# Weight sums of each pair's last product queued behind an earlier split on VectorE, in all pairs but the last gated one

## The chip, the cores and the metric

The kernel runs on one core of a Trainium2 chip. A time is the device time of one execution in microseconds, of the slowest core where there are several; here there is one. TensorE (PE, with its weight loads PEld), VectorE (DVE), ScalarE (ACT) and GpSimd (POOL) each take their instructions in a fixed order; SyncE (SP) issues nearly all transfers (DMAs), also in a fixed order. An instruction waits at the head of its engine's queue until what it needs is there, and everything behind it on that engine waits too.

## What is computed

One layer of a decoder over 512 tokens of width 2048, all in float32:

```
p = rms_norm(x) @ w_in                       # 2048 x 6160
A = gated linear attention (4 heads, chunks of 64)
B = dilated sliding-window attention (8 heads, three dilations)
x = x + concat(A, B) @ w_out                 # 2048 x 2048
h = rms_norm(x)
x = x + (silu(h @ w_gate) * (h @ w_up)) @ w_down    # 2048 x 5632 twice, 5632 x 2048
```

Nearly all of the work is in the large products with weights that stand in memory: w_in, w_out, w_gate, w_up and w_down.

## The kernel before

**Products.** The large products are made by a fast scheme with seven products instead of eight for each two-by-two block: P1, P5, P6, P3, P7, P2 and P4 in this order. A *pair* is one such block product: two column blocks of 512 of a weight (or of w_gate and w_up), with 2048 rows (1408 for the last third of w_down). Its weight is cut in quarters named a, b, c, d; each quarter is loaded in four *groups* (g = 0 to 3; three in the last two pairs) of 128 x 1024 elements, 512 KB. P1, P3 and P2 use the quarters a, d and c as they are. P5, P6, P7 and P4 need differences, which VectorE writes over one of the two: P5 makes a = b - a, P6 makes a = d - a, P7 makes b = d - b, and P4 makes a = c - a. I call each of these 128 x 1024 subtractions a *sum*, after the code. They are line 230, in `Pair.source`.

**Splits.** Float32 products are made of a high and a low part of both factors. For each *item* (one product, one group) ScalarE casts the weight tile to its high part `wh` (line 320), VectorE subtracts that to get the low part `wl` (line 324, the *split*), and TensorE then runs twelve matmuls of 128 x 512 (line 364): eight on `wh`, then four on `wl`. `wh` and `wl` have two buffers each. So a pair has 28 items, 28 casts, 28 splits and 16 sums.

**The stream.** `stream` runs over the items of 24 pairs: four pairs of the input projection, one gated pair of it, two pairs with w_out, eleven pairs with w_gate and w_up (the gated pairs, j = 0 to 10), and six pairs with w_down. I number them 0 to 23: 0 to 4 w_in, 5 and 6 w_out, 7 to 17 w_gate and w_up, 18 to 23 w_down. (A pair before these is written out by hand.) At item k it traces the cast of item k+1, the sum of item k+2 and the split of item k+1, then the matmuls of item k. Work of other kinds (attention, the norm, the factors of the next stage) is traced between the matmuls in small steps, by `step`.

**Who sets the order.** That is only the order in which the program is traced. A scheduler then sets the order on each engine, and issues an instruction early when its inputs are there by the scheduler's own reckoning. A sum of P4 needs the quarter c, whose load needs a free one of the twelve weight buffers, and the quarter a after the split of P6. So the scheduler puts it as much as ten splits ahead of its own item's split: among the splits of P3 and P7, where it is traced among those of P2. `tc.issue_after(ins)` tells the scheduler to place what is traced in a block behind `ins` on that engine; it sets the order alone and adds no semaphore. Before the change it is used in one place around the sums: in the gated pair of the input projection (pair 4), whose sums stay behind the latest step of the attention's softmax (`behind_heads`).

**Buffers.** Sixteen weight tiles of a pair go through the twelve buffers of `wpool`: the four c tiles take the buffers of d, and b of the next pair takes those of c. A c tile is free when both the split of P2 and the sum of P4 have read it, an a tile after the split of P4. The load of the next tile waits for that at the head of SyncE's queue.

**Handover from pair 6 to pair 7.** Pair 6 makes the last columns of `x` after attention. VectorE adds the residual (lines 277 and 1445), ScalarE squares and scales it (1478, 1453), TensorE transposes it (1166), ScalarE copies it out (1177), SyncE stores it to `xn_d` (1181) and loads it back as `top` and `r` (1227, 1281), and from these VectorE and ScalarE make the factors `AA` and `AS` (178, 179) of pair 7. The third item of pair 7, (P1, group 2), needs the factor made of the first `top`.

Of the kernel before, what the change touches and what calls it, by code (L numbers as in the profile page):

```python
# [2 lines left out]

# [28 lines left out]
PRODUCTS = ("P1", "P5", "P6", "P3", "P7", "P2", "P4")  # L32
# [76 lines left out]
def block_kernel(ctx: ExitStack, tc: tile.TileContext, ins, out):  # L109
    nc = tc.nc  # L110
# [18 lines left out]
    def nm(s):  # L129
        uid[0] += 1  # L130
        return f"{s}_{uid[0]}"
# [34 lines left out]
    class Operand:  # L166


        def __init__(self, groups):
            self.groups = groups  # L170
            self.t = {}
# [16 lines left out]
    def folded(w):  # L188

        return w.rearrange("p (b a) -> p a b", b=2)  # L190
# [8 lines left out]
    class Pair:  # L199


        def __init__(
            self, op, rows, w1, w2, final, step, scale=None, before=None, products=PRODUCTS
        ):
            self.op, self.rows, self.w1, self.w2 = op, rows, w1, w2
            self.final, self.step, self.scale, self.before = final, step, scale, before
            self.q, self.dst, self.held = {}, {}, {}
            self.products = products
            self.closes = {**CLOSES}
            if products is FIRST_CLOSED:  # L210
                self.closes["P1"] = self.closes.pop("P2")
# [7 lines left out]
        def source(self, prod, g):  # L219

            if prod in SINGLE:
                t = self.quarter(SINGLE[prod], g)
                if prod == "P2" and self.products is FIRST_CLOSED:
                    self.q.pop(("c", g))
                return t
            one, two = SUMS_OF[prod]
            src = self.quarter(two, g)
            minuend = self.quarter(one, g)
            with self.behind_heads():
                nc.vector.tensor_tensor(src, minuend, src, op=ALU.subtract)  # L230
            return src

        def behind_heads(self):

            if self.final is final_gate and "head" in recent:
                return tc.issue_after(recent["head"])
            return ExitStack()

        def accs(self):
# [51 lines left out]
        def end(self, prod):  # L291
# [6 lines left out]
            else:  # L298
                self.held[prod] = self.seeds(src, int(prod == "P5"))

    def stream(pairs):


        items, asks = [], {}
        for p in pairs:
            for part in p.products:
                groups = [int(g) for g in part[3:] or "0123"[: p.op.groups]]
                if groups[-1] == p.op.groups - 1:
                    asks[len(items)] = p
                items += [(p, part[:2], g) for g in groups]  # L310
        last = len(items) - 1
        sources, high, low = {}, {}, {}

        def total(k):
            p, prod, g = items[k]
            sources[k] = p.source(prod, g)

        def first_part(k):
            high[k] = hpool.tile([P, 2, 512], F32R, name=nm("wh"), tag="wh")
            nc.scalar.copy(high[k], sources[k])  # L320

        def second_part(k):
            low[k] = hpool.tile([P, 2, 512], F32R, name=nm("wl"), tag="wl")
            nc.vector.tensor_tensor(  # L324
                low[k], sources.pop(k), high[k].bitcast(F32), op=ALU.subtract
            )

        def ensure(k):

            p, prod, g = items[k]  # L330
            finish(lambda: (COMBO[prod], g) in p.op.t)

        total(0)
        first_part(0)
        total(1)
        second_part(0)
        for k, (p, prod, g) in enumerate(items):
            if g == 0:
                if prod == p.products[0] and p.before:
                    p.before()  # L340
                p.begin(prod)
            if k in asks:
                p.ask(prod)
            now[0] = k
            run_soon()
            ensure(min(k + 1, last))
            if k < last:
                first_part(k + 1)
            if k + 2 <= last:
                total(k + 2)  # L350
            if k < last:
                second_part(k + 1)
            a = p.op.t[COMBO[prod], g]
            fresh = prod in ("P1", "P5", "P2")
            h, l = high.pop(k), low.pop(k)
            order_ = [
                (m, w, terms, jj, hl)
                for w, terms in ((h, (0, 1)), (l, (0,)))
                for jj in range(2) for m in range(2) for hl in terms
            ]  # L360
            if k == last:
                order_.sort(key=lambda o: o[0])
            for i, (m, w, terms, jj, hl) in enumerate(order_):
                nc.tensor.matmul(  # L364
                    p.dst[prod][m], a[:, jj, hl, m * P : (m + 1) * P], folded(w[:, jj, :]),
                    start=fresh and g == 0 and len(terms) == 2 and jj == 0 and hl == 0,
                    stop=g == p.op.groups - 1 and len(terms) == 1 and jj == 1,
                    skip_group_check=not fresh,
                )
                if i == 7:  # L370
                    p.step()
            if g == p.op.groups - 1:
                p.end(prod)
# [7 lines left out]
    def run_soon():  # L381
        for d in list(soonest):
            d[0] -= 1
            if d[0] <= 0:
                soonest.remove(d)
                d[1]()
# [120 lines left out]
    def step(n=1):  # L507
        for d in list(deferred):
            d[0] -= 1
            if d[0] <= 0:  # L510
                deferred.remove(d)
                d[1]()
        if any(d[2] for d in deferred):
            return
        spent = 0.0
        while spent + 1e-6 < n:
            if spent:
                run_soon()
            cost = advance()
            if cost is None:  # L520
                break
            spent += cost
        return spent
# [19 lines left out]
    def finish(ready):  # L543

        while not ready():
            hurry[0] = True
            run_soon()
            assert advance() is not None
        hurry[0] = False

    def paced(counts):
        counts = iter(counts)
        return lambda: step(next(counts, 1))
# [67 lines left out]
    def bias_tables():  # L621


        rel = work("T", (33, 8))
        nc.gpsimd.memset(rel[32:33, :], 1.0)
        load(rel[0:32, :], ins["rel_bias"])
        parts = []
        for c0, cn, t0, t1 in ((0, 512, "v", "qT"), (512, NB - 512, "oT", "kT")):
            oh = work(t0, (33, cn))
            load(oh, ins["onehot"][:, c0 : c0 + cn])  # L630
            parts.append((c0, cn, oh, t1))
        yield
        yield
        for c0, cn, oh, t1 in parts:
            bp = bank()
            nc.tensor.matmul(bp[:8, :cn], rel, oh, start=True, stop=True)
            lv = work(t1, (8, cn))
            nc.vector.tensor_copy(lv, bp[:8, :cn])
            store(bias_d[:, c0 : c0 + cn], lv)
        yield  # L640
        load(rep_d, bass.AP(tensor=bias_d.tensor, offset=0, ap=[[NB, 8], [0, P], [1, NB]]))
        yield
# [759 lines left out]
    def pair(*args, **kw):  # L1402
        pairs.append(Pair(*args, **kw))

    pair(opx, rows_in, col(1536), col(1024), final_proj("va1", "va0"), rate((22, 1), (6, 0.6)),
         row_scale, before=lambda: background.extend([gates(), bias_tables()]))
# [5 lines left out]
         products=FIRST_CLOSED)  # L1412
# [256 lines left out]
    def before_ffn(j):  # L1669
        if j == 10:  # L1670
            background.append(down_jobs(0))

    for j in range(11):
        c = slice(512 * j, 512 * j + 512)
        pair(
            opn, rows_n, w_gate[:, c], w_up[:, c], final_ffn(j),
            paced(paces.get(j, ())), tok_scale, before=lambda j=j: before_ffn(j),
        )


# [46 lines left out]
    for i in range(3):  # L1727
        g0 = 4 * i
        rows_d = [(512 * (g0 + g), 512 * (g0 + g) + 256) for g in range(opd[i].groups)]
        for np_ in range(2):  # L1730
# [5 lines left out]
                before=(lambda i=i: background.append(down_jobs(i + 1))) if lead else None,  # L1736
# [6 lines left out]
    for engine in ("act", "dve", "pe"):  # L1743
        behind.enter_context(tc.issue_after(recent[engine]))
    pairs[1].before = behind.close
    stream(pairs)
    drain()

# [34 lines left out]
```

## Time and profile before

| what | value |
|---|---|
| median of 3 runs | 1935.62 us (1932.67 to 1936.36) |
| the profiled execution's own time | 1928.62 us |
| its span, first to last instruction | 1926.8 us |
| granted TensorE clock, mean | 0.999 |
| TensorE busy | 1900.7 us (99%) |
| VectorE busy | 1684.6 us (87%) |
| ScalarE busy | 1070.6 us (56%) |
| transfers | 362.01 MB, 188 GB/s over the span |

The profiled execution took 1928.62 us, 1.8 us more than its span and 7.0 us less than the median. A matmul's busy time is longer than its share of the engine: matmuls are pipelined, so 99% busy hides short gaps, and one has to look at the starts. The timeline merges equal neighbours: "x8" is eight instructions, with the start of the first and the time until the last has ended, and in brackets the idle time of the engine before them with what ended it. VectorE's 128 x 1024 instructions are shown with 1.22 us, but follow each other 1.14 us apart.

### The profile page before, as it was taken

The page shows a single profiled execution, that of the slowest core. Times are in us where ns is not written, and L with a number is a line of the kernel's source. Part 1 is how long each engine was busy: PE and PEld are TensorE (multiplying, and loading weights), DVE is VectorE, ACT ScalarE, POOL GpSimd, SP SyncE. Part 2 cuts the span into 40 slices and gives each one's busy share as a digit, 9 for nine tenths or more (in the row PEclk, how much of TensorE's full clock was granted, in tenths as well). Part 3 has the DMA queues.
Part 4 walks back from the last instruction along what each step waited for, and adds up shares of the span by engine and source line. Part 5 has one row for each costly group of instructions (what it writes and reads, how often), then busy time and mean ns, then how long its engine had stood idle before and what let it go on. Part 6 is the DMA issues. An engine that isn't in the chain of part 4 may idle for free.

```text
span 1926.8 us, 25472 instructions
## 1 busy us (share of the span) xinstructions
PE 1900.7 (99%) x8986; PEld 1642.7 (85%) x8986; DVE 1684.6 (87%) x1915; ACT 1070.6 (56%) x1550; POOL 58.0 (3%) x80
## 2 busy tenths in 40 slices
PE   8999999999999999999999999999999999999999
PEld 7888888888888878888888888888888888888887
DVE  8997887877999799978878879879879989989987
ACT  8564564567776676544544444544446546546543
POOL 1000221010000010000000000000000000000000
PEclk9999999999999999999999999999999999999999
DMA  8458365476767594564564554564556785955761
GB/s 284 132 167 277 102 190 153 137 209 196 221 228 245 188 310 158 154 191 147 154 191 144 151 186 132 158 190 123 166 184 188 215 283 175 277 205 173 247 219 66
DMA packets 341800, 362.01 MB, mean 188 GB/s; under 512 B 132790, under 2 KB 202623, under 8 KB 341672
## 3 DMA queue, kind: packets, MB, share of 16 engines
q1 hardware_dynamic: 341320, 360.17, 59.6%
q8 instruction: 70, 1.15, 0.2%
q14 instruction: 58, 0.48, 0.1%
q10 hardware_dynamic: 352, 0.21, 0.0%
HBM read 298.16 MB, written 64.51 MB: 188 GB/s over the span
## 4 chain that ended last, share of the span: by engine, by line
PE 68%; DVE 11%; issue 3%; DMA 3%; ACT 1%; POOL 0%; DVEq 0%; SPq 0%; ACTq 0%; POOLq 0%
PE acc L364 66%; DVE wl L324 5%; DVE wa L230 2%; DVE AS L179 1%; PE bank L1033 1%; PE bank L999 1%; DVE wb L230 1%; ACT wh L320 0%; DVE AA L179 0%; DMA wc<-in_w_gate 0%; PE bank L1026 0%; DVE seed L281 0%; DMA top<-xn_d 0%; DMA r<-xn_d 0%; DMA x_d<-seed 0%
## 5 line engine op out<-in xcount | busy, mean ns | idle before, releaser
L364 PE MATMUL acc<-wh,AS 128*128 128x512 f32 x3008 | 710.9, 379 | 0.0
L364 PEld LDWEIGHTS acc<-wh,AS 128*128 128x128 f32 x3008 | 568.3, 189 | 81.1 <-issue 0.2
L320 ACT CAST wh<-wa 128x1024 fp32r<-128x1024 f32 x376 | 394.0, 1049 | 400.3 <-PE acc L364 369.7
L364 PE MATMUL acc<-wh,AA 128*128 128x512 f32 x2256 | 535.8, 380 | 2.1 <-ACT wh L320 1.8
L324 DVE TENSOR_TENSOR wl<-wa,wh 128x1024 fp32r<-128x1024 f32 x376 | 456.8, 1217 | 53.0 <-ACT wh L320 46.1
L364 PEld LDWEIGHTS acc<-wh,AA 128*128 128x128 f32 x2256 | 426.8, 189 | 64.6 <-ACT wh L320 3.3
L364 PE MATMUL acc<-wl,AS 128*128 128x512 f32 x1504 | 398.0, 386 | 7.3 <-DVE wl L324 7.1
L364 PEld LDWEIGHTS acc<-wl,AS 128*128 128x128 f32 x1504 | 279.5, 189 | 60.5 <-DVE wl L324 20.0
L364 PE MATMUL acc<-wl,AA 128*128 128x512 f32 x1128 | 295.1, 384 | 1.7 <-DVE wl L324 1.5
L364 PEld LDWEIGHTS acc<-wl,AA 128*128 128x128 f32 x1128 | 211.3, 189 | 36.4 <-DVE wl L324 6.4
L320 ACT CAST wh<-wb 128x1024 fp32r<-128x1024 f32 x94 | 98.6, 1048 | 125.3 <-PE acc L364 108.5
L320 ACT CAST wh<-wc 128x1024 fp32r<-128x1024 f32 x94 | 98.4, 1047 | 113.1 <-PE acc L364 108.7
L230 DVE TENSOR_TENSOR wa<-wc,wa 128x1024 f32<-128x1024 f32 x94 | 114.5, 1222 | 49.6 <-DMA wc<-in_w_gate 30.1
L320 ACT CAST wh<-wd 128x1024 fp32r<-128x1024 f32 x94 | 98.5, 1048 | 99.1 <-PE acc L364 96.9
L324 DVE TENSOR_TENSOR wl<-wc,wh 128x1024 fp32r<-128x1024 f32 x94 | 114.6, 1219 | 35.8 <-ACT wh L320 34.3
L324 DVE TENSOR_TENSOR wl<-wd,wh 128x1024 fp32r<-128x1024 f32 x94 | 114.4, 1220 | 16.2 <-ACT wh L320 11.9
L324 DVE TENSOR_TENSOR wl<-wb,wh 128x1024 fp32r<-128x1024 f32 x94 | 113.6, 1217 | 6.7 <-ACT wh L320 6.5
L230 DVE TENSOR_TENSOR wa<-wb,wa 128x1024 f32<-128x1024 f32 x94 | 113.5, 1219 | 2.0 <-DMA wb<-in_w_down 1.1
L230 DVE TENSOR_TENSOR wb<-wd,wb 128x1024 f32<-128x1024 f32 x94 | 114.6, 1219 | 0.6
L230 DVE TENSOR_TENSOR wa<-wd,wa 128x1024 f32<-128x1024 f32 x94 | 112.9, 1219 | 0.0
L281 DVE SCALAR_TENSOR_TENSOR seed<-acc,rs,seed 128x512 f32<-128x512 f32 x96 | 70.5, 746 | 23.3 <-PE acc L364 23.3
L265 ACT ACTIVATE seed<-acc,rs 128x512 f32<-128x512 f32 x96 | 60.6, 680 | 0.8 <-PE acc L364 0.8
(309 smaller groups left out, 1313.2 us busy)
## 6 DMA issues: line engine op xcount, KB each, us to landing
wa<-in_w_gate SPq DMA_DIRECT2D x44, 512.0 KB, 3.8
wb<-in_w_up SPq DMA_DIRECT2D x44, 512.0 KB, 4.5
wd<-in_w_up SPq DMA_DIRECT2D x44, 512.0 KB, 3.5
wc<-in_w_gate SPq DMA_DIRECT2D x44, 512.0 KB, 3.4
wc<-in_w_in SPq DMA_DIRECT2D x32, 512.0 KB, 4.1
wa<-in_w_in SPq DMA_DIRECT2D x24, 512.0 KB, 5.8
wb<-in_w_in SPq DMA_DIRECT2D x24, 512.0 KB, 5.7
wd<-in_w_in SPq DMA_DIRECT2D x24, 512.0 KB, 6.5
```

Source lines behind the costliest of these rows:

```text
L179: nc.vector.tensor_tensor(low, src, high.bitcast(F32), op=ALU.subtract)
L230: nc.vector.tensor_tensor(src, minuend, src, op=ALU.subtract)
L265: nc.scalar.activation(halves(t), unfolded(src[m]), AF.Copy, scale=self.scale(half, m))
L281: nc.vector.scalar_tensor_tensor(halves(seed[m]), unfolded(src[m]), self.scale(half, m), halves(seed[m]), op0=ALU.mult, op1=ALU.add,)
L320: nc.scalar.copy(high[k], sources[k])
L324: nc.vector.tensor_tensor(low[k], sources.pop(k), high[k].bitcast(F32), op=ALU.subtract)
L364: nc.tensor.matmul(p.dst[prod][m], a[:, jj, hl, m * P : (m + 1) * P], folded(w[:, jj, :]), start=fresh and g == 0 and len(terms) == 2 and ...
L999: nc.tensor.matmul(lp[:, :n], qh[:, b * P : (b + 1) * P], kh[:, :n], start=True, stop=True)
L1033: nc.tensor.matmul(op, vh[:, k, :], lgs[b][:, k * P : (k + 1) * P], start=(k == 0), stop=(k == b))
```

## The change

The splits of the stream are remembered in a queue of six. When a sum of P4 is traced for item k+2, the oldest of these six is the split of item k-5, seven items up the stream from the sum's own. The sum is now placed behind that split in VectorE's order. The gated pair of the input projection keeps its own rule, and the pair with j = 10, the last of w_gate and w_up (pair 17), is left out with `runs_ahead`. No instruction, load or buffer is added or removed.

```
+    splits = deque(maxlen=6)
...
         def second_part(k):
             low[k] = hpool.tile([P, 2, 512], F32R, name=nm("wl"), tag="wl")
-            nc.vector.tensor_tensor(
+            splits.append(nc.vector.tensor_tensor(
                 low[k], sources.pop(k), high[k].bitcast(F32), op=ALU.subtract
-            )
+            ).ins)
...
-            with self.behind_heads():
+            with self.held_back(prod):
                 nc.vector.tensor_tensor(src, minuend, src, op=ALU.subtract)
             return src
 
-        def behind_heads(self):
+        def held_back(self, prod):
 
             if self.final is final_gate and "head" in recent:
                 return tc.issue_after(recent["head"])
+            if prod == "P4" and not self.runs_ahead and len(splits) == splits.maxlen:
+                return tc.issue_after(splits[0])
             return ExitStack()
...
     for j in range(11):
         c = slice(512 * j, 512 * j + 512)
         pair(
             opn, rows_n, w_gate[:, c], w_up[:, c], final_ffn(j),
             paced(paces.get(j, ())), tok_scale, before=lambda j=j: before_ffn(j),
+            runs_ahead=j == 10,
         )
```

In the order of the built program, the four sums of P4 of a gated pair stood 10 splits ahead of their own items' splits, behind the splits of (P3, 1), (P3, 2), (P3, 3) and (P7, 0); they now stand 6 ahead, behind (P7, 1), (P7, 2), (P7, 3) and (P2, 0). The scheduler moves other instructions with them: in pair 6 the last two sums stand only 2 and 1 splits ahead of their own, and what feeds pair 7 is reordered on VectorE, ScalarE, TensorE and SyncE. In pairs 4, 5, 7 and 17 the places of the sums stay as they were.

More of the change, by code (lines that the diff above doesn't have):

```diff
@@ L1 @@
 import math
+from collections import deque
 from contextlib import ExitStack
@@ L202, in __init__ @@
         def __init__(
-            self, op, rows, w1, w2, final, step, scale=None, before=None, products=PRODUCTS
+            self, op, rows, w1, w2, final, step, scale=None, before=None, products=PRODUCTS,
+            runs_ahead=False,
         ):
@@ L208, in __init__ @@
             self.products = products
+            self.runs_ahead = runs_ahead
             self.closes = {**CLOSES}
@@ L228, in source, with held_back @@
             minuend = self.quarter(one, g)
-            with self.behind_heads():
+            with self.held_back(prod):
                 nc.vector.tensor_tensor(src, minuend, src, op=ALU.subtract)
             return src
-        def behind_heads(self):
+        def held_back(self, prod):
             if self.final is final_gate and "head" in recent:
                 return tc.issue_after(recent["head"])
+            if prod == "P4" and not self.runs_ahead and len(splits) == splits.maxlen:
+                return tc.issue_after(splits[0])
             return ExitStack()
@@ L299, in end @@
                 self.held[prod] = self.seeds(src, int(prod == "P5"))
+    splits = deque(maxlen=6)
     def stream(pairs):
@@ L323, in second_part @@
             low[k] = hpool.tile([P, 2, 512], F32R, name=nm("wl"), tag="wl")
-            nc.vector.tensor_tensor(
+            splits.append(nc.vector.tensor_tensor(
                 low[k], sources.pop(k), high[k].bitcast(F32), op=ALU.subtract
-            )
+            ).ins)
         def ensure(k):
@@ L1677, in block_kernel @@
             paced(paces.get(j, ())), tok_scale, before=lambda j=j: before_ffn(j),
+            runs_ahead=j == 10,
         )
```

## The prediction

> **What bounds the kernel now.** I read the groups on the page first, then the waits, the windows by pair, and the timelines of VectorE and TensorE where the two meet.
>
> ```profile
> span 1926.8 us, 25472 instructions
> PE 1900.7 (99%) x8986; PEld 1642.7 (85%) x8986; DVE 1684.6 (87%) x1915; ACT 1070.6 (56%) x1550; POOL 58.0 (3%) x80
> ...
> L364 PE MATMUL acc<-wl,AS 128*128 128x512 f32 x1504 | 398.0, 386 | 7.3 <-DVE wl L324 7.1
> ...
> L230 DVE TENSOR_TENSOR wa<-wc,wa 128x1024 f32<-128x1024 f32 x94 | 114.5, 1222 | 49.6 <-DMA wc<-in_w_gate 30.1
> ```
>
> The last group is the sums of P4: 94 of them, and VectorE stands idle for 49.6 us before them, waiting for c. The waits say the same, and what TensorE loses to late splits:
>
> ```profile
> DVE wa L230 <- DMA wc<-in_w_gate: 30.1, 29, 2.6
> ...
> PEld acc L364 <- DVE wl L324: 26.4, 51, 1.6
> ...
> PE acc L364 <- DVE wl L324: 8.6, 18, 1.2
> ```
>
> So the whole of what late splits cost is between 8.6 us (TensorE idle) and 26.4 us (weight loads held, part of it hidden). That caps any gain at 1.4% of the span. Now by stage; the columns are the window, its length, and busy time of PE, PEld, DVE, ACT and POOL:
>
> ```profile
> 861.30:934.00 72.70, 72.70 (x338) 63.32 (x337) 62.36 (x63) 35.18 (x39) 0.00 (x0) 1.00 0.54 163
> 654.00:672.00 18.00, 18.00 (x93) 15.89 (x92) 10.29 (x10) 11.82 (x21) 0.00 (x0) 1.00 0.68 227
> 672.00:708.00 36.00, 34.35 (x165) 28.19 (x164) 34.67 (x47) 28.87 (x51) 0.00 (x0) 1.00 0.89 311
> ```
>
> The first is a whole gated pair (pair 9). 72.70 us for 28 items is 2.596 us an item or 0.216 us a matmul, and TensorE has no gap: it is the bound there, VectorE has 10 us to spare. The other two are halves of pair 6: VectorE idle for 7.7 of 18 us, then busy for 34.67 of 36.
>
> The start of the low-part matmuls shows the margin of a split. An item's eight high-part matmuls take 8 x 0.216 = 1.73 us; if its low part starts later than that, the split was late. Pair 9, first VectorE, then TensorE:
>
> ```profile
> 896.20 1.23 DVE L230 TENSOR_TENSOR wa<-wc,wa 128x1024 f32<-128x1024 f32 x1 [2.03 <-DMA wc<-in_w_gate]
> 897.34 1.22 DVE L324 TENSOR_TENSOR wl<-wd,wh 128x1024 fp32r<-128x1024 f32 x1
> ...
> 904.70 1.22 DVE L230 TENSOR_TENSOR wa<-wc,wa 128x1024 f32<-128x1024 f32 x1 [0.39 <-DMA wc<-in_w_gate]
> 905.84 1.22 DVE L324 TENSOR_TENSOR wl<-wb,wh 128x1024 fp32r<-128x1024 f32 x1
> ```
>
> ```profile
> 905.48 1.89 PE L364 MATMUL acc<-wh,AS 128*128 128x512 f32 x8
> 907.21 1.03 PE L364 MATMUL acc<-wl,AS 128*128 128x512 f32 x4
> ```
>
> The sum waits 2.03 us for c, and the splits behind it are late by what the sums wait. The split of (P7, 1) ends at 905.84 + 1.22 = 907.06, TensorE wants it at 907.21: 0.15 us to spare. In pair 9 the waits still cost nothing.
>
> **The change, part by part.** Nothing is added or removed, so VectorE's busy time, the transfers and ScalarE's and TensorE's work stay. No semaphore is added. POOL's order is untouched.
>
> *Gain: splits no longer queue behind a sum that waits for c.* Where the margin was gone, in pair 12, pair 15 and pair 18:
>
> ```profile
> 1121.91 1.22 DVE L324 TENSOR_TENSOR wl<-wb,wh 128x1024 fp32r<-128x1024 f32 x1
> ```
>
> ```profile
> 1121.03 1.89 PE L364 MATMUL acc<-wh,AS 128*128 128x512 f32 x8
> 1123.18 1.13 PE L364 MATMUL acc<-wl,AS 128*128 128x512 f32 x4 [0.26 <-DVE wl L324]
> 1124.15 1.89 PE L364 MATMUL acc<-wh,AS 128*128 128x512 f32 x8
> 1126.42 1.13 PE L364 MATMUL acc<-wl,AS 128*128 128x512 f32 x4 [0.38 <-DVE wl L324]
> ...
> 1342.94 1.89 PE L364 MATMUL acc<-wh,AS 128*128 128x512 f32 x8
> 1344.90 1.13 PE L364 MATMUL acc<-wl,AS 128*128 128x512 f32 x4
> ...
> 1558.86 1.89 PE L364 MATMUL acc<-wh,AS 128*128 128x512 f32 x8
> 1561.94 1.13 PE L364 MATMUL acc<-wl,AS 128*128 128x512 f32 x4 [1.20 <-DVE wl L324]
> ```
>
> ```profile
> 1559.53 1.23 DVE L230 TENSOR_TENSOR wa<-wc,wa 128x1024 f32<-128x1024 f32 x1 [2.18 <-DMA wc<-in_w_down]
> ```
>
> Lateness is start minus start minus 1.73: 0.42 + 0.54 + 0.23 + 1.35 = 2.5 us. In each a sum of P4 stands right ahead of the split. They go; lower bound 1.35 us (the one of pair 18, whose wait is 2.18), if the others come back elsewhere. What is late next in these stretches: the same four sums now lie among the closing additions of P7 and P2. An item there holds at most one split, one sum and one addition (0.68 us, as at 703.99 below), 1.14 + 1.14 + 0.68 = 2.96 us against 2.596, twice in six items, so a split falls behind by 0.7 us at the most. With two buffers the next item's split may begin when an item begins, so it has 2.596 + 1.73 - 1.22 = 3.1 us, less what is left of ScalarE's cast by then. Cost: nothing, hidden by that margin; without it 0.7 us a pair.
>
> *Loss: pair 6.* Rows of VectorE, TensorE, SyncE and ScalarE at the handover to pair 7:
>
> ```profile
> 670.80 1.23 DVE L230 TENSOR_TENSOR wa<-wc,wa 128x1024 f32<-128x1024 f32 x1 [2.75 <-DMA wc<-in_w_out]
> ...
> 703.99 0.68 DVE L1445 TENSOR_TENSOR seed<-seed,k 128x512 f32<-128x512 f32 x1
> ```
>
> ```profile
> 704.29 1.89 PE L364 MATMUL acc<-wh,AA 128*128 128x512 f32 x8
> ...
> 708.69 1.99 PE L364 MATMUL acc<-wh,AA 128*128 128x512 f32 x8
> ...
> 713.12 1.03 PE L364 MATMUL acc<-wl,AA 128*128 128x512 f32 x4
> 715.98 3.64 PE L364 MATMUL acc<-wh,AA 128*128 128x512 f32 x8 [1.84 <-ACT wh L320]
> ...
> 720.71 1.89 PE L364 MATMUL acc<-wh,AA 128*128 128x512 f32 x8
> ...
> 728.18 1.13 PE L364 MATMUL acc<-wl,AS 128*128 128x512 f32 x4 [0.40 <-DVE wl L324]
> ...
> 732.86 1.13 PE L364 MATMUL acc<-wl,AS 128*128 128x512 f32 x4 [0.95 <-DVE wl L324]
> ```
>
> ```profile
> 707.87 1.18 SPq L1227 DMA_DIRECT2D top<-xn_d x2
> ...
> 710.12 0.56 SPq L1181 DMA_DIRECT2D xn_d<-PT  x1
> ```
>
> ```profile
> 714.37 0.62 ACT L178 CAST AA<-top 128x512 fp32r<-128x512 f32 x1 [2.10 <-DMA top<-xn_d]
> ```
>
> Three of the pair's sums leave the half with 7.7 us idle (their waits there, 2.75 us the longest, cost little) for the half that has 1.33 us left: 3 x 1.14 = 3.4 us. I take 3.0 of it as delay at the end, so the last residual addition starts at 706.9 instead of 703.99. The squares, scaled copies, transposes and stores hang on it: the last store goes from 710.12 to 713.1. The last splits are late too, so TensorE's next pair starts later than 708.69, by an estimate of 2 us, which lies within the 5.5 us below.
>
> Then SyncE's order. Before, the loads of the first `top` (707.87) stand ahead of the two stores; in the new order they stand behind them, and behind weight loads that wait for the sums of P4 groups 2 and 3. So they go at 713.1 + 0.56 = 713.7, 5.8 us later. From issue to the cast it was 714.37 - 707.87 = 6.5 us; so the cast comes at 720.2, then 0.62 for it and 0.7 for the low part: TensorE starts that item at 721.5 instead of 715.98, **+5.5 us**. Lower bound: a load of 3.4 us (the shortest from the weight loads below), 718.4, +2.4. I take the row of the same load. While TensorE waits, VectorE catches up: the gaps ahead of the two late low parts behind it (0.40 us at 728.18, 0.95 us at 732.86) should go, **-1.35**; if the loads of `r`, later too, hold them, 0.
>
> ```profile
> wc<-in_w_gate SPq DMA_DIRECT2D x44, 512.0 KB, 3.4
> ...
> 717.00:718.00 1.00, 1.00 (x4) 0.82 (x3) 1.00 (x2) 0.90 (x2) 0.92 (x2) 0.50 0.74 235
> ```
>
> The second row is a window in which the granted clock was 0.50: the item from 715.98 to 720.71 took 4.7 us where 2.6 is usual. A gap of 1.84 us was enough, so I count no second price for a longer gap. [...]
>
> [...]
>
> *Other pairs.* In pairs 4, 5, 7 and 17 the sums stand as before: 0. In the attention pairs 0 to 3 and in 19 to 21 the sums move within stretches with room; between a gain and a loss of 0.5 us, taken as 0.
>
> **The sum.** On the profiled execution: -2.5 + 5.5 - 1.35 = +1.65, 1928.62 to 1930.3 us. That execution lies 7.0 us under the median, so the timed runs lose more somewhere. The gated pairs are one likely place: 0.15 us of margin is all that hides a late c. An estimate of 0.2 us for each of ten such pairs is 2.0 us that the change saves only there. 1935.62 + 1.65 - 2.0 = **1935.3 us**.
>
> **Rivals.**
> - *Faster: late c costs more in timed runs.* If c lands half a microsecond later, each of nine gated pairs (8 to 16) loses that less 0.15, about 0.45 with the waits of its other sums: 4.0 us, all saved. With the handover at its lower bound (+2.4 - 1.35): 1935.62 - 2.5 - 4.0 + 1.05 = 1930.2. For it: 30.1 us of waits, and margins of 0.15. Against: in the profiled execution only pairs 12 and 15 lost any.
> - *Slower: the handover at its full price.* +5.5 with nothing given back, and a gain of the lower bound alone: 1935.62 + 5.5 - 1.35 = 1939.8. It decides from 3.9 us net. For it: SyncE's order is fixed by the program, not by luck. Against: the longer wait lets VectorE catch up.
> - *It does nothing.* The splits still wait for ScalarE's casts and the margins hide the rest, in pair 6 as well: 1935.6.
>
> **Chances.** 0.2% is 3.9 us, about what can be told from no change here. Forecast 0.40 and nothing 0.10, both within; faster rival 0.28; slower rival 0.22. So faster 0.28, same 0.50, slower 0.22. The range 1929 to 1940 reaches to both rivals and a little past; the likeliest case by itself spans 1931.8 to 1939.5.
>
> **What would show it.** The group of P4's sums: idle time before it from 49.6 us to under 10, and nothing late at the low-part matmuls of P3 and P7 in pairs 8 to 18. VectorE in the first half of pair 6 less busy, its last residual addition about 3 us later, the first `top` issued after the two stores, and a gap of TensorE ahead of the third item of pair 7 of 4 us or more where it was 1.84. I am wrong if the handover does not get longer, if the sums find new waits in P7 and P2, or if the gated pairs shorten by more than 0.5 us each.

## The result, and the profile after

The changed kernel takes 1926.65 us (median of 6 runs, 1925.08 to 1929.33). The kernel before took 1935.76 us beside it (6 runs, 1932.67 to 1937.54). The ratio is 0.9958, with a 95% interval of 0.9947 to 0.9970: 0.42% faster, and 2.4 us below the low end of the predicted range. The profiled execution of after took 1926.97 us. That of before had taken 1928.62 us, which is less than any timed run of it here. The two profiles differ by 1.7 us only, the timed medians by 9.1 us; where the other 7 us are is what the experiments had to find.

The page of after, first its head, then the low-part matmuls on AS and the sums of P4 (group; count; busy and mean; idle before and what ended it):

```profile
span 1925.1 us, 25455 instructions
...
PE 1897.7 (99%) x8986; PEld 1642.8 (85%) x8986; DVE 1682.6 (87%) x1915; ACT 1070.7 (56%) x1550; POOL 60.0 (3%) x80
...
L371 PE MATMUL acc<-wl,AS 128*128 128x512 f32 x1504 | 397.3, 386 | 4.5 <-DVE wl L331 4.1
...
L233 DVE TENSOR_TENSOR wa<-wc,wa 128x1024 f32<-128x1024 f32 x94 | 114.2, 1220 | 0.0
```

VectorE does the same work, and its 49.6 us of idle time before the sums are gone: no sum finds its c still on the way. The waits of TensorE for late splits went from 26.4 and 8.6 us to these (total, count, longest):

```profile
PEld acc L371 <- DVE wl L331: 21.5, 45, 1.7
...
PE acc L371 <- DVE wl L331: 6.0, 9, 1.5
```

The places that were late in pairs 12 and 18 of the timeline, TensorE:

```profile
1121.30 1.89 PE L371 MATMUL acc<-wh,AS 128*128 128x512 f32 x8
1123.02 1.03 PE L371 MATMUL acc<-wl,AS 128*128 128x512 f32 x4
...
1560.43 1.89 PE L371 MATMUL acc<-wh,AS 128*128 128x512 f32 x8
1562.16 1.03 PE L371 MATMUL acc<-wl,AS 128*128 128x512 f32 x4
```

Each low part now starts 1.72 or 1.73 us after its high part, as it should. In pair 18 it was 3.08 us.

The windows of pair 6 by halves (VectorE is the third busy time), and its handover to pair 7 as VectorE, SyncE, ScalarE and TensorE show it:

```profile
656.90:674.90 18.00, 18.00 (x93) 15.89 (x92) 8.68 (x8) 13.10 (x22) 0.00 (x0) 1.00 0.76 242
674.90:710.90 36.00, 33.97 (x159) 27.64 (x159) 35.27 (x46) 26.66 (x47) 0.00 (x0) 1.00 0.91 298
```

```profile
708.35 0.70 DVE L1452 TENSOR_TENSOR seed<-seed,k 128x512 f32<-128x512 f32 x1
```

```profile
713.56 0.56 SPq L1188 DMA_DIRECT2D xn_d<-PT  x1
714.22 2.79 SPq L1234 DMA_DIRECT2D top<-xn_d  x4
```

```profile
719.75 0.62 ACT L179 CAST AA<-top 128x512 fp32r<-128x512 f32 x1 [2.49 <-DMA top<-xn_d]
```

```profile
717.62 0.38 PE L1173 MATMUL bank<-mats,L 128*128 128x128 f32 x2
720.42 2.29 PE L371 MATMUL acc<-wh,AA 128*128 128x512 f32 x8 [2.42 <-ACT AA L179]
...
735.72 1.13 PE L371 MATMUL acc<-wl,AS 128*128 128x512 f32 x4 [1.50 <-DVE wl L331]
```

VectorE does less in the first stretch and more in the second, the first loads of `top` stand behind the stores, and TensorE waits 2.42 us where it waited 1.84. All of that was foreseen; the size was not. Pair 6 starts 2.99 us later in this trace than in that of before (628.79 against 625.80), so that against its start the last residual addition is 1.4 us later (79.56 against 78.19), the loads are issued 3.4 us later, the cast comes 2.4 us later and the third item of pair 7 1.4 us later.

The next table has the time between the first matmuls of two pairs, in us, for all profiled executions of the two kernels: the first and the repeated ones, and those of the last group of experiments (b, c, d). They come from more than one chip; b, c and d of before and b of after are from the same one. "Time" is that of the whole execution.

| execution | time | to pair 0 | 0 to 5 | 6 and 7 | 8 to 16 | 17 | 18 to 21 | 22 to end |
|---|---|---|---|---|---|---|---|---|
| before, first | 1928.62 | 100.7 | 525.1 | 162.7 | 655.9 | 73.5 | 296.0 | 112.8 |
| before, repeated | 1929.76 | 101.1 | 526.3 | 161.4 | 656.1 | 73.6 | 296.7 | 112.8 |
| before b | 1934.06 | 101.5 | 525.5 | 162.1 | 660.1 | 73.6 | 296.7 | 112.8 |
| before c | 1936.07 | 100.9 | 526.0 | 161.7 | 660.5 | 73.7 | 298.7 | 112.8 |
| before d | 1935.83 | 101.1 | 525.2 | 164.6 | 658.1 | 73.5 | 298.7 | 112.8 |
| after, first | 1926.97 | 101.5 | 527.2 | 162.6 | 654.4 | 73.6 | 293.0 | 112.8 |
| after, repeated | 1930.24 | 100.5 | 527.3 | 167.1 | 654.4 | 73.6 | 292.8 | 112.8 |
| after b | 1925.21 | 102.0 | 526.0 | 161.8 | 654.4 | 73.6 | 292.8 | 112.8 |

### The profile page after: what moved, and what is told of

It is laid out like the page before. It is cut to its first block, busy times and chain, and to the rows that moved or that the text cites. A ratio compares the mean times of both kernels' runs of the same rounds, so it can differ in the third digit from the quotient of the medians.

```text
span 1925.1 us, 25455 instructions
## 1 busy us (share of the span) xinstructions
PE 1897.7 (99%) x8986; PEld 1642.8 (85%) x8986; DVE 1682.6 (87%) x1915; ACT 1070.7 (56%) x1550; POOL 60.0 (3%) x80
## 4 chain that ended last, share of the span: by engine, by line
PE 81%; DVE 11%; issue 3%; DMA 3%; ACT 1%; SPq 0%; DVEq 0%; ACTq 0%
PE acc L371 75%; DVE wl L331 4%; DVE wa L233 2%; PE acc L439 2%; DVE AS L180 1%; DVE AA L180 1%; DMA wa<-in_w_in 1%; PE bank L1040 1%; PE bank L1006 1%; DMA wc<-in_w_in 1%; DVE wl L423 0%; PE bank L792 0%; DVE seed L286 0%; DMA wb<-in_w_in 0%; DMA wa<-in_w_gate 0%
```

## The experiments

Two theories. A: c lands late by an amount that changes from execution to execution; in the old order each late c holds the splits behind it, in the new order none does. B: what the timed runs lose lies elsewhere (attention, handover, clock). In the variants, one line chooses the pairs whose sums are held (`self.n` is the number of the pair). The pair of the input projection with its own rule (pair 4) keeps it in all of them:

```diff
-            if prod == "P4" and not self.runs_ahead and len(splits) == splits.maxlen:
+            if prod == "P4" and self.n in HOLD and len(splits) == splits.maxlen:
```

**The kernel before once more.** No edit.

> The kernel before, unchanged, for a second profiled execution and more times. Theory A (c lands later in most executions than in the one that was profiled, and each gated pair with the old order pays for it): times of 1933 to 1937 us, and, if this profile falls among them, pairs 8 to 16 longer than 72.7 us by 0.3 to 1 us each, with a sum of P4 that waits for c right ahead of each late split. Rival B (the timed runs lose their time elsewhere: attention, the handover from pair 6 to pair 7, or the start): pairs 8 to 16 stay at 72.7 us and the excess of 5 us or more lies in pairs 0 to 7 or 18 to 23.

1931.91 us (12 runs, 1929.32 to 1936.49) beside 1931.87 for the kernel before, ratio 1.0000 (0.9992 to 1.0009). It is 4 us faster here than in the first runs. The profile, at 1929.76 us, is again from the low end and settles nothing: pairs 8 to 16 have 656.1 us.

**Held in the gated pairs alone.**

```diff
-    splits = deque(maxlen=6)
+    splits, HOLD = deque(maxlen=6), set(range(8, 17))
```

> The sums of P4 are held in the gated pairs 8 to 16 alone; everywhere else they stand where they stood before. Theory A: most of the gain stays, 1927 to 1930 us against 1935.6 (1.5 us from pairs 12 and 15 in the profile, and some 5 us that only the timed runs showed). Rival B: 1.5 us at the most, 1934 us.

1929.91 us against 1931.87, ratio 0.9993 (0.9985 to 1.0002). Pairs 8 to 16 fall to 654.4 us, the figure of the changed kernel. On this chip that is worth about 2 us, which the interval can't tell from nothing. The time lies within theory A's range only because the kernel before is 4 us faster here; as a gain it is nearer to B's 1.5 us.

**Held everywhere but in the gated pairs.**

```diff
-    splits = deque(maxlen=6)
+    splits, HOLD = deque(maxlen=6), set(range(24)) - set(range(8, 18))
```

> The reverse: the sums are held everywhere but in the gated pairs 8 to 16. Theory A: it gains little, 1932 to 1935 us: pairs 18 to 21 give 3 us, pairs 4 and 5 take back 1.8, and the loss of the gated pairs stays. Rival B: most of the gain, 1927 to 1930 us.

1927.97 us, ratio 0.9982 (0.9973 to 0.9991): 3.9 us, twice what the gated pairs gave alone. Pairs 18 to 21 take 292.8 us instead of 296.7. Theory A's 1932 to 1935 us missed and theory B's number came out; B had named pairs 18 to 23 as a place, but no cause there.

**Held as in the changed kernel, but not in pair 6.**

```diff
-    splits = deque(maxlen=6)
+    splits, HOLD = deque(maxlen=6), set(range(24)) - {6, 17}
```

> Held as in the changed kernel, but not in pair 6, so that the first loads of top stand ahead of the stores as before. If the handover costs nothing in the changed kernel, as the two profiles say (pairs 6 and 7 together -0.13 us): the time of the changed kernel, 1926 to 1928 us. If it does cost what the prediction took, hidden by luck in the profiled execution: 1 to 4 us less, 1923 to 1926 us.

1924.96 us (1924.53 to 1925.72), ratio 0.9965 (0.9953 to 0.9977). Pairs 6 and 7 take 161.6 us. The second expectation held: the time is 1.7 us under the 1926.65 of the changed kernel in the first runs. The changed kernel wasn't run on this chip, and pair 6 alone is released, so this points to a cost of holding it, of 1 to 2 us.

**The changed kernel on the next chip.** No edit.

> The changed kernel once more, so that the variants stand beside it on one chip. Theory C (the gain is the sum of parts that add up: gated pairs about -2.0 us, pairs 18 to 21 about -5, pair 6 and its handover +1.2, attention pairs about +1): -4 to -7 us against the kernel before on the same chip. If the gain is one of luck in the handover's clock instead: about 2 us, with single times spread by 4 us or more.

1926.61 us (11 runs, 1925.76 to 1930.24) against 1931.91, ratio 0.9975 (0.9966 to 0.9984). The kernel before is 4 us faster here than in the first runs, the changed one takes the same 1926.6. So what differs between them is something that only the old order pays for. The profiled execution is the slowest of the runs, and shows where the changed kernel pays: pairs 6 and 7 at 167.1 us. SyncE, ScalarE and TensorE there, and windows of 2 us with the granted clock in the third column from the right:

```profile
714.38 2.95 SPq L1234 DMA_DIRECT2D top<-xn_d  x4
```

```profile
721.60 0.62 ACT L179 CAST AA<-top 128x512 fp32r<-128x512 f32 x1 [4.51 <-DMA top<-xn_d]
```

```profile
722.27 2.08 PE L371 MATMUL acc<-wh,AA 128*128 128x512 f32 x4 [4.44 <-ACT AA L179]
```

```profile
722.00:724.00 2.00, 1.73 (x4) 1.41 (x5) 1.75 (x3) 2.00 (x4) 0.00 (x0) 0.50 0.90 303
724.00:726.00 2.00, 2.00 (x6) 1.55 (x6) 2.00 (x4) 0.81 (x2) 0.00 (x0) 0.50 0.88 267
```

The load took 7.2 us from issue to cast (5.5 in the first profile of after), TensorE's gap was 4.44 us, and half clock behind it cost again. Pairs 6 and 7 are some 4 us longer than in the first profile of before, close to the +4.15 of the prediction, but in part by luck: a second stretch of half clock is in it, which the prediction had ruled out.

**Held in the gated and the w_down pairs.**

```diff
-    splits = deque(maxlen=6)
+    splits, HOLD = deque(maxlen=6), set(range(8, 17)) | set(range(18, 24))
```

> Held in the gated pairs 8 to 16 and in the pairs of w_down, 18 to 23, alone; pairs 0 to 7 stand as before. Theory C: the two parts that gain without the two that cost, so 1 to 2 us under the changed kernel and at or a little under the version without pair 6 (1924 to 1925 us where that had 1925). Rival: moving the sums in the attention pairs helps in the timed runs as well (late c there too); then this is 1 us or more over the version without pair 6.

1924.49 us (1923.54 to 1925.83) against 1931.91, ratio 0.9963 (0.9950 to 0.9975); the changed kernel beside it has 1926.61. It is the fastest version here, and its 5 runs spread by 2.3 us where the 11 of the changed kernel spread by 4.5: what the sums of pairs 0 to 6 gain by being held is less than it costs.

**Held in the w_down pairs alone.**

```diff
-    splits = deque(maxlen=6)
+    splits, HOLD = deque(maxlen=6), set(range(18, 24))
```

> Held in the pairs of w_down alone. Theory C: the larger part of the gain, -4 to -5.5 us against before, though the profiles show 3.0 to 3.9 us there, because the wait of pair 18 for c changes from execution to execution (lateness 1.35, 2.3 and 1.2 us in three profiles of the old order). Rival (each part gives what the first profile showed): -3 us.

1927.77 us, ratio 0.9977 (0.9968 to 0.9986): -4.1 us. Theory C's number came out. With the -2.0 of the gated pairs, from another chip, that makes -6.1 where both together measured -7.4, so the parts add up within what the medians can tell.

**Held one item instead of four.**

```diff
-    splits = deque(maxlen=6)
+    splits, HOLD = deque(maxlen=9), set(range(8, 17)) | set(range(18, 24))
```

> As the version held in the gated and w_down pairs, but held behind the split only nine back instead of six: each sum of P4 stands one item later than before (2.6 us), not four. If c is late by no more than the waits in the profiles (2.0 to 2.8 us), one item is enough: the time is that of six splits, within 1 us, and the late low parts of pairs 12, 15 and 18 are gone as well. If c is at times later than that, this lies between: 1 to 4 us slower than six splits, with a wider spread.

1926.45 us, ratio 0.9974 (0.9964 to 0.9983), 2 us behind the hold of four items. For pairs 8 to 16 one item was enough in this execution (654.4 us), for pairs 18 to 21 it wasn't: 294.7 us against 292.8. The second expectation came out.

**c made late on purpose, old order.**

```diff
-        load(t, w[r0 : r0 + 256, :].rearrange("(j p) n -> p j n", p=P))
+        with tc.issue_after(recent["load"]) if "load" in recent else ExitStack():
+            recent["load"] = load(t, w[r0 : r0 + 256, :].rearrange("(j p) n -> p j n", p=P)).ins
...
+                if name == "c" and 8 <= self.n <= 16:
+                    r0 = self.rows[g][1]
+                    with tc.issue_after(recent["load"]):
+                        recent["load"] = store(
+                            dram([128, 512], nm("beside")), w[r0 : r0 + 128, :]
+                        ).ins
```

> The kernel before, with c made late on purpose: in the gated pairs 8 to 16 SyncE also copies 256 KB of w_gate within DRAM ahead of each load of c, and the load of c is queued behind it. Theory A (a c that lands later is paid for in each gated pair of the old order, with 0.15 us of margin): pairs 8 to 16 grow to 73.5 to 75 us where they have 72.71, 8 to 20 us in all. Rival (ScalarE's casts or free buffers set the splits as much as c does): under 3 us.

1939.45 us against 1931.22, ratio 1.0036 (1.0024 to 1.0048): +8.2 us. Pairs 8 to 16 take 661.8 us, where the five executions of before have 655.9 to 660.5; three of the nine reach the 73.5 us that theory A expected of each. The edit does more than delay c: it also ties every weight load to the one before it, in all pairs. And of the 9.6 us between this profiled execution (1939.38) and the repeated one of before, 5.7 lie in pairs 8 to 16, 2.3 in pairs 18 to 21, which have no copies, and 2.0 ahead of pair 8. So by itself this run doesn't price a late c; it is the one to compare with the next.

**The same copies, sums held.**

```diff
-        load(t, w[r0 : r0 + 256, :].rearrange("(j p) n -> p j n", p=P))
+        with tc.issue_after(recent["load"]) if "load" in recent else ExitStack():
+            recent["load"] = load(t, w[r0 : r0 + 256, :].rearrange("(j p) n -> p j n", p=P)).ins
...
+                if name == "c" and 8 <= self.n <= 16:
+                    r0 = self.rows[g][1]
+                    with tc.issue_after(recent["load"]):
+                        recent["load"] = store(
+                            dram([128, 512], nm("beside")), w[r0 : r0 + 128, :]
+                        ).ins
...
-    splits = deque(maxlen=6)
+    splits, HOLD = deque(maxlen=6), set(range(8, 17)) | set(range(18, 24))
```

> The same copies in the version that holds the sums in the gated and w_down pairs. Theory A: the sums stand 10 us later, so c may be late by more than that: pairs 8 to 16 stay at 72.7 us and the time within 1 us of 1924.5. Rival (the copies cost by their traffic, not by c): it grows as much as the kernel before does.

1925.46 us, ratio 0.9963 (0.9949 to 0.9977); pairs 8 to 16 take 654.4 us, as without the copies. The sums of P4 in the two kernels, first the old order, then the new:

```profile
L237 DVE TENSOR_TENSOR wa<-wc,wa 128x1024 f32<-128x1024 f32 x94 | 114.5, 1223 | 58.6 <-DMA wc<-in_w_gate 38.1 <-DMA wc<-in_w_in 10.4 <-DMA wc<-in_w_down 6.9
```

```profile
L240 DVE TENSOR_TENSOR wa<-wc,wa 128x1024 f32<-128x1024 f32 x94 | 114.2, 1220 | 13.8 <-DMA wc<-in_w_in 10.6 <-DMA wc<-in_w_out 3.2
```

The two kernels have the same copies and the same tied loads, ran on one chip, and differ in the place of the sums alone: 1939.45 us against 1925.46, with 7.4 us of it in pairs 8 to 16 and 6.2 in pairs 18 to 21. So it isn't the traffic: in pairs 8 to 16 of the old order, what is over 2.6 us an item lies, but for the 0.19 us at (P6, 1) that every profile has, at (P3, 3), (P7, 0) and (P7, 1), whose splits stand right behind a sum of P4. The held kernel is 1.0 us over its own 1924.49 from another chip. VectorE's wait for c from w_gate, 38.1 us, is only 8 us over the 30.1 of the first profile, so little lateness is enough once the margin of 0.15 us is gone.

**The changed kernel without its exemption.**

```diff
-    splits = deque(maxlen=6)
+    splits, HOLD = deque(maxlen=6), set(range(24))
```

> The changed kernel without its exemption: the sums of pair 17 (the last gated one) are held too. Two of its sums then move from ahead of the splits of P7 to behind them, and TensorE keeps its 72.7 us there, so theory C says within 1 us of the changed kernel, pair 17 at 73.5 us. Rival: the held sums meet the closing additions and the background splits of the first w_down operand; pair 17 or 18 grows by 1 us or more.

1928.51 us, ratio 0.9985 (0.9975 to 0.9994), so about 2 us worse than the changed kernel by the two ratios, from two chips and with intervals that overlap. The rival's number came out: pair 17 takes 75.3 us instead of 73.6. Its cause did not; the place is a third one, as SyncE, ScalarE and TensorE of this kernel show.

```profile
1500.97 4.60 SPq L186 DMA_DIRECT2D wb<-in_w_down  x3
1505.81 0.37 SPq L1583 DMA_DIRECT2D qT<-p_d  x1
```

```profile
1511.22 0.62 ACT L179 CAST AA<-qT 128x512 fp32r<-128x512 f32 x1 [4.21 <-DMA qT<-p_d]
1511.75 1.04 ACT L327 CAST wh<-wa 128x1024 fp32r<-128x1024 f32 x1
```

```profile
1512.84 1.99 PE L371 MATMUL acc<-wh,AA 128*128 128x512 f32 x8 [1.02 <-ACT wh L327]
```

A load of `qT` for the next operand stands behind three weight loads that wait for buffers, ScalarE waits 4.21 us for it, and the cast of the P4 item queues behind. It is what the prediction feared for `top` in pair 6, one engine further on.

**Held seven items instead of four.**

```diff
-    splits = deque(maxlen=6)
+    splits, HOLD = deque(maxlen=3), set(range(8, 17)) | set(range(18, 24))
```

> Held in the gated and w_down pairs, but behind the split only three back: the sums stand among the splits of P2, seven items later than before. If the splits alone matter, as with six: 1924.5 us within 1 us. If the sums then come too close to their own casts, or crowd the closing additions of P7 and P2 (a sum, a split and an addition are 2.96 us in an item of 2.596): a few tenths in each of 13 pairs, 2 to 6 us slower.

1924.93 us (1923.93 to 1926.29), ratio 0.9959 (0.9946 to 0.9972). No loss: the additions do not crowd the sums, and the depth between four and seven items makes no difference that these times show.

**Three more executions of before, one of after.** No edit, on a chip where the kernel before took 1937.49 us in one run.

> The kernel before, profiled again. Two profiled executions of it took 1928.6 and 1929.8 us, though its times on the first chip were 1932.7 to 1937.5. If an execution of 1931 us or more is caught: theory A has pairs 8 to 16 and 18 longer (each late split right behind a sum that waits for c); theory H (the clock) has one or two more stretches of half clock with low parts late by nothing, at the handover or elsewhere, 1.7 us each.

> As the run before it, another execution: how pairs 12, 15, 18, 20 and the handover differ from execution to execution of the same kernel. Theory A: their sum moves by 2 us or more between executions. Theory H: they stay within 0.5 us and the place of the half clock moves.

> As the two before it, a third execution. Theory A: pairs 8 to 21 together differ by 2 us or more among the executions; theory H: by less than 0.5 us.

> The changed kernel, a third execution, for the handover: two profiles of it have pairs 6 and 7 at 162.6 and 167.1 us, the second with two stretches of half clock there. Theory H: the handover is at 162.6 us without a stretch of half clock in it, some 164 with one, 167 with two; pairs 8 to 21 as in both profiles within 0.3 us.

1934.06, 1936.07 and 1935.83 us for before, 1925.21 us for after. These are executions of the kind that was timed, and the table has them. Against the changed kernel they lose 3.7 to 6.1 us in pairs 8 to 16 and 3.8 to 5.8 us in pairs 18 to 21. In pairs 8 to 16 all of the loss lies at the items (P3, 2), (P7, 0) and (P7, 1): in the three executions of before, 42 items there are late by 0.07 us or more, and each has its split right behind a sum of P4 that waited for c. The groups, VectorE and TensorE of the second one, pair 14:

```profile
L230 DVE TENSOR_TENSOR wa<-wc,wa 128x1024 f32<-128x1024 f32 x94 | 114.5, 1223 | 56.7 <-DMA wc<-in_w_gate 36.0 <-DMA wc<-in_w_in 10.4 <-DMA wc<-in_w_down 7.0
```

```profile
1271.14 1.23 DVE L230 TENSOR_TENSOR wa<-wc,wa 128x1024 f32<-128x1024 f32 x1 [1.43 <-DMA wc<-in_w_gate]
1272.29 1.22 DVE L324 TENSOR_TENSOR wl<-wb,wh 128x1024 fp32r<-128x1024 f32 x1
```

```profile
1271.06 1.89 PE L364 MATMUL acc<-wh,AS 128*128 128x512 f32 x8
1273.56 1.13 PE L364 MATMUL acc<-wl,AS 128*128 128x512 f32 x4 [0.61 <-DVE wl L324]
```

The split ends at 1273.51, 0.72 us after TensorE wanted it (1271.06 + 1.73), behind a sum that waited 1.43 us. The first profile of before had no late split in pair 14. And pair 18 of the same execution, with a window that has its clock:

```profile
1565.33 1.22 DVE L230 TENSOR_TENSOR wa<-wc,wa 128x1024 f32<-128x1024 f32 x1 [2.39 <-DMA wc<-in_w_down]
1566.47 1.22 DVE L324 TENSOR_TENSOR wl<-wd,wh 128x1024 fp32r<-128x1024 f32 x1
```

```profile
1563.66 1.89 PE L364 MATMUL acc<-wh,AS 128*128 128x512 f32 x8
1567.74 1.82 PE L364 MATMUL acc<-wl,AS 128*128 128x512 f32 x4 [2.19 <-DVE wl L324]
1569.36 2.93 PE L364 MATMUL acc<-wh,AS 128*128 128x512 f32 x8
1572.12 1.03 PE L364 MATMUL acc<-wl,AS 128*128 128x512 f32 x4
```

```profile
1568.00:1570.00 2.00, 2.00 (x6) 1.60 (x6) 2.00 (x3) 0.82 (x1) 0.00 (x0) 0.51 0.46 140
```

The late c costs 2.35 us (1567.74 - 1563.66 - 1.73), and half clock behind the gap about 1.7 us more: the eight matmuls from 1569.36 to 1572.12 take 2.76 us instead of 1.73, and the four ahead of them 1.62 instead of 0.86. Pair 18 has 78.7 us there and 74.5 in the changed kernel, which is the sum of both. Theory A holds for pairs 8 to 16 and pair 18, and theory H for a part of pair 18.

Pairs 19 to 21 are another case. They lose 1.7 us in each of the three (220.0 us against 218.3), as much as in the first profile of before, and little of it is a sum that waits for c. In pair 20 of that first profile, VectorE and TensorE:

```profile
1668.90 1.23 DVE L230 TENSOR_TENSOR wa<-wb,wa 128x1024 f32<-128x1024 f32 x1 [1.12 <-DMA wb<-in_w_down]
```

```profile
1672.31 1.89 PE L364 MATMUL acc<-wh,AA 128*128 128x512 f32 x8
1674.79 1.13 PE L364 MATMUL acc<-wl,AA 128*128 128x512 f32 x4 [0.59 <-DVE wl L324]
```

The sum is one of P5 that waits for b, and the low part of (P1, 2) is 0.75 us late (1674.79 - 1672.31 - 1.73). The hold removes this too; which of the moved instructions or loads does it was not tried.

Of the changed kernel's handover, theory H came near: 161.8 us in the third execution, which has no half clock there (H had 162.6), where the repeated one with two stretches has 167.1. In that third execution the load took 4.0 us from issue to cast:

```profile
713.76 2.65 SPq L1234 DMA_DIRECT2D top<-xn_d  x4
```

```profile
717.75 0.62 ACT L179 CAST AA<-top 128x512 fp32r<-128x512 f32 x1 [0.93 <-DMA top<-xn_d]
```

## Why the prediction was wrong

The means of the three typical executions of before and the three of after differ by 7.8 us (1935.3 against 1927.5). By stretch: to pair 0 +0.2, pairs 0 to 5 +1.3, pairs 6 and 7 +1.0, pairs 8 to 16 -5.2, pair 17 -0.1, pairs 18 to 21 -5.2.

- *"In 19 to 21 the sums move within stretches with room [...] taken as 0", and 1.35 us for pair 18*: this is the step that failed most. It gave pairs 18 to 21 a gain of 1.35 us; they gained 3.0 us in the first profile already and 5.2 by the means. Pairs 19 to 21 gave 1.7 us: the late low parts of pairs 19 and 20 were in the trace of before and weren't listed. Pair 18 gave 3.4: its wait was priced from one execution (1.35 us) and is 2.35 us in another, and the half clock that its gap can set off was no term of the sum.
- *"An estimate of 0.2 us for each of ten such pairs is 2.0 us"*: with the 1.2 us of pairs 12 and 15 it made 3.2 us for the gated pairs; the three executions have 5.2. It counted ten pairs where nine could gain, and the 0.2 came from no row. The 7.0 us between the profiled execution and the median were the better measure: of the 6.7 us by which the three executions are slower than the first profile, 3.6 lie in pairs 8 to 16 and 2.0 in pairs 18 to 21. One of the prediction's own signs of being wrong came true here: the gated pairs shortened by 0.57 us each (5.2 over nine), not by 0.5 at most.
- *The handover, +5.5 - 1.35 = +4.15*: -0.1 us between the first profiles, +1.0 us by the means of three. The mechanism was right and the size wrong. The last residual addition came 1.4 us later, not 2.9; the loads 3.4 us later, not 5.8; from issue to cast they took 5.5 us in the first profile and 4.0 and 7.2 in the others, not the 6.5 of one row; and the first matmul followed the cast by 0.67 us (719.75 to 720.42), not by the 1.3 of the sum. The gap of 4 us or more was there in one execution of three (2.42, 4.44 and 0.86 us). The -1.35 did not come: the late low parts at 728.18 and 732.86 became one of 1.50 us. And the trace of before had paid 1.7 us of half clock there, which the first profile of after did not.
- *"I count no second price for a longer gap"*: wrong once in three. The gap of 4.44 us paid two stretches of half clock.
- *Pairs 0 to 5 at 0 within 0.5 us*: +1.3 us by the means, 1.0 of it in pair 4 (107.1 against 106.1), whose own sums do not move. This may be chance in part: the version held from pair 8 on, where these pairs stand as before, has 527.2 us there in its profile, as much as the changed kernel. Why it grows wasn't tried.
- *What is late next in P7 and P2, "cost: nothing"*: right. Pairs 8 to 16 take 654.4 us, 9 x 72.71, in all three executions and in every variant that holds them, with four items or seven.
- *No time in pair 17 for the exemption*: right, 73.6 us on both sides; without it 75.3.

The rival "late c costs more in timed runs" was the true case. Its 4.0 us, with the 1.2 of pairs 12 and 15, are the 5.2 us that the gated pairs gave, and its +1.05 for the handover is the +1.0 of the means. Its 1930.2 us was too slow by pairs 18 to 21, where it too had 1.35 us for 5.2. Whether the first timed runs of before split just like the three executions isn't shown: the only profile beside them is the fast one.

## What to carry to other kernels

Where one execution is profiled and others are timed, compare their times first: a profile 7 us below the median shows a kernel at its best, and the waits that it hides with 0.15 us to spare can be the price in the others. An in-order engine should not have a wait for a transfer ahead of work that another engine needs at once; moved back by four items, 10 us here, the wait for c was gone in the held pairs of every profile. The same move costs where loads of the next stage are queued behind buffers that it frees later, so hold only in the stages that gain: 1924.5 instead of 1926.6 us here.

## What the runs showed of the hardware

Half clock comes in stretches of one length. By the mean clock of windows of 0.5 us, the stretch at the handover of the first profile of before lasts from 716.86 to 720.27, 3.41 us, that of pair 18 above 3.41 us too, the one in the second profile of after 6.83 us, twice that; each 3.41 us at the granted clock of 0.50 costs 1.7 us where TensorE has work. The gap ahead doesn't decide by its length: 1.84 us was followed by half clock in one execution, 2.42 us in another was not:

```profile
718.00:720.00 2.00, 0.00 (x0) 0.00 (x0) 0.00 (x0) 0.25 (x1) 1.78 (x4) 1.00 1.00 349
```

In three traces with two stretches, the starts lie whole multiples of one step apart: 716.86 and 1925.18 us in the first profile of before (1208.32 us, 354 steps), 43.10 and 1923.84 us in the first of after (1880.74 us, 551 steps), 718.51 and 1568.43 us in execution d of before (849.92 us, 249 steps). The step that fits all three is 3.4133 us, and a stretch by itself is 3.413 us long (716.859 to 720.272 us in the trace of before). With a grid of this step drawn through each execution's own stretches, the two gaps look different. Here are the step ahead of half clock in the first profile of before, and the two that share the gap of 2.42 us in the first of after (length, then TensorE's busy time; the granted clock stands third from the right):

```profile
713.45:716.86 3.41, 1.49 (x6) 0.74 (x5) 1.74 (x5) 2.10 (x3) 0.21 (x1) 1.00 1.02 360
```

```profile
715.53:718.94 3.41, 2.33 (x11) 1.48 (x9) 2.44 (x4) 1.73 (x4) 0.72 (x3) 1.00 1.05 372
718.94:722.35 3.41, 1.90 (x8) 1.37 (x9) 1.95 (x3) 2.60 (x4) 2.13 (x3) 1.00 0.95 315
```

TensorE was idle for 1.92 us of the first step, and for 1.08 and 1.51 us of the other two, because the gap lies across a boundary. Worked out in the same way for the first profiles of before and after, from 5 us on, the full-clock steps with 1.92 (713.45 us in before), 1.99 (39.69 in after), 2.20 (1921.76 in before) and 2.54 us of idle time (1920.43 in after) were followed by half clock; the one with 1.95 (41.02 in before) was not, nor any with 1.61 or less. Fifteen of the other traces have half clock between 5 and 1900 us. Windows of 2 us, over some nine tenths of each, bound the idle time of a step there: half clock begins 20 times, always behind a step that can hold some 1.8 us or more, and no full-clock step that can hold 2.0 us went without it. So in these runs half clock came behind some 1.8 to 2 us or more of idle time within one step, and where the gap falls on the grid differs from execution to execution: a boundary of the grid lies 0.06 us after the first instruction in the first profile of before, 2.14 us after it in the first of after, 1.71 us after it in execution d.

Also new was how much the same load differs: `top`, 4.0, 5.5 and 7.2 us from issue to cast in three executions of the changed kernel.
